# Squares, high-part products and weight splits in the pooling mixer of a two-block network

## The chip, the cores and the metric

The kernel runs on one core of a Trainium2 chip. Its time is the device time of one execution in microseconds; a figure for a kernel is the median of its runs. Each kernel has one profiled execution besides, and all times inside the kernel are on that execution's clock, counted from the start of its span.

## The reference

Two blocks of layers follow each other on 256 tokens of width 1024 in float32. The first block (two layers of mixed attention) isn't touched. The second has two layers; in front of the 256 tokens it puts 16 learned ones, so it works on 272. Its first layer is the stage that matters here:

```python
f = swiglu(rmsnorm(h, ffn_norm_pre[0, 0]), ...)
h = h + 0.5 * rmsnorm(f, ffn_norm_post[0, 0])
hn = rmsnorm(h, mix_norm_pre[0])
m = causal_multiscale_pool(hn, pool_w[0], pool_b[0], pool_scale[0])
h = h + rmsnorm(m, mix_norm_post[0])
f = swiglu(rmsnorm(h, ffn_norm_pre[0, 1]), ...)
```

The pool splits the 1024 channels into four groups of 256. Group g takes, for each token, the mean over the last 2, 4, 8 or 16 tokens, subtracts the token itself, and multiplies the difference by a 256 x 256 matrix of its own. A bias is added and a scale per channel applied.

## The kernel before

Activations lie with channels on the 128 partitions and the 272 tokens along the row: the state is eight tiles `h[0..7]`, and a product's operand is eight pairs `xh[k]`, `xl[k]`. A float32 value is split in a high part (`xh`, `hi`) that TensorE reads in its fast float32 form, and a low part (`xl`, `lo`), the rest. A product of two such values is three products: low weight by high operand, high weight by high operand, and high weight by low operand.

Weights come in chunks of 128 x 1024, in the order in which they are used. SyncE's queue loads a chunk into one of four `raw` buffers (L233); ScalarE casts it to `hi` (L250) and VectorE subtracts to get `lo` (L251). Both together are called a split. Near a border between stages splits are held back (`held`) and issued later by `release`, which asks the scheduler to place them behind given instructions. Each engine runs its instructions in the order that a scheduler gave them when the program was built; `issue_after` is a wish for that order.

Between a feed-forward layer and the pool stands `boundary` (from L941). It has the sums of squares of the layer's output, makes the scale `s` from them (logarithm and exponential on ScalarE, in two halves of the tokens), and then makes the tiles one after the other: VectorE multiplies the layer's output `fg[k]` by `s` (L958, L964) and adds it to `h[k]` (L972); ScalarE makes `xh[k]` (L387) and VectorE `xl[k]` (L388). Tile 0 has a shorter way: VectorE makes its `xh` directly (L965), and `xl` (L969) follows behind the addition to `h` (L968). The squares of `h`, wanted for the norm ahead of the pool, are made by ScalarE: those of tiles 0, 2 and 4 into `sums`, those of 1, 3 and 5 into `sq`, which GpSimd adds to the former (L979); tiles 6 and 7 have `sums` of their own.

`pool_mixer` (from L1122) multiplies first and takes the means afterwards. For each of the eight tiles it makes nine products: three token tiles (128, 128 and 16 tokens) by the three products of parts, with the tile as the stationary operand (L287 low part of the tile, L288 low part of the weights, L289 both high). The results are rows by token; two groups, so four tiles, fill one set of three PSUM banks, and each set is copied to `zt` in SBUF (L1185, L1187). Between the tiles TensorE sums the squares over channels with a matrix of 1/1024 (`squares`, L1163): a set is three products of 2 columns, one for each token tile, and each is seen as two passes. When the last set is done, ScalarE makes the scale of the norm from it by logarithm and exponential (`rt_pool`, `rc_pool`, L934 and L935), and `bands` multiplies the banded matrices of the means by it: `mb[0]` (L1214) and `mb[2]` (L1218) on VectorE, `mb[1]` (L1216) on ScalarE. Then comes the mix: for each of the eight channel tiles three products of `zt` by these matrices (L1195, L1197, L1199) bring the data back to channels on partitions, and `branch_out` evicts the bank: ScalarE takes the squares (`facc`, `fq`, L1015), VectorE the values (`fg`, L1016). GpSimd adds the squares of the first five tiles (L1021) into `facc`. Four products with the matrix of means (L1031) add all of it, over tile 5, `facc`, tile 6 and tile 7 in that order, and the next boundary starts with its scale.

Two splits are released in the middle of the tiles, behind the last `xl` (`self.tiles_done`); in the trace they run on ScalarE and VectorE while TensorE is at tiles 5 to 7.

## Time and profile before

| | |
|---|---|
| runs | 1266.91, 1268.29, 1268.59 us |
| median | 1268.29 us |
| profiled execution | 1266.44 us, span 1264.7 us |
| mean granted TensorE clock | 0.995 |
| TensorE busy | 1237.0 us, 98% of the span |
| VectorE, ScalarE, GpSimd busy | 850.3, 699.6, 204.7 us |
| read from HBM | 200.16 MB, 159 GB/s over the span |

Busy times overlap, and a busy TensorE isn't always at its peak. The stage of the pool mixer is read in the timelines: each row has the start, the time, engine, line and operation, output <- input with their shapes, and in brackets how long the engine had been idle before it and what released it. Rows of one line that follow each other are merged (x6); their time then runs from the first start to the last end. Float32 products of full width, as in the sums of squares, stand as two passes each.

### The profile page before, as it was taken

The numbers are of one execution on the slowest core, as the hardware profiler recorded it, in microseconds if no ns is written. First come the engines' busy times: TensorE is split into PE (matmuls) and PEld (weight loads), VectorE is DVE, ScalarE is ACT, GpSimd is POOL, SyncE is SP. The second block draws the span as 40 slices with busy tenths as digits, with TensorE's granted clock in tenths as the row PEclk, the third lists the DMA queues.
The fourth block names the chain that finished last, engine by engine and source line by source line (L and its number), as shares of the span: only waits on it lengthen the run. The fifth ranks groups of instructions, "written<-read, shape, count | busy, mean of one in ns | idle before, by whom it ended". The sixth has DMA issues, their size and how long they took to land.

```text
span 1264.7 us, 23255 instructions
## 1 busy us (share of the span) xinstructions
PE 1237.0 (98%) x9105; PEld 1161.2 (92%) x9105; DVE 850.3 (67%) x1468; ACT 699.6 (55%) x1233; POOL 204.7 (16%) x308
## 2 busy tenths in 40 slices
PE   8999999999999999899999999999999999999998
PEld 6778897789999999799999999999999988999986
DVE  7988759777666644887664467665456886776652
ACT  6878658586544533565444346444335665665541
POOL 5201010012211112321111122110121002321100
PEclk9999999999999999999999999999999999999999
DMA  7642443335554554146555526554534533475550
GB/s 261 202 160 91 167 167 115 119 125 179 202 179 168 182 167 167 34 139 228 171 180 169 182 84 218 186 181 173 178 117 152 166 117 118 153 240 176 185 181 34
DMA packets 59662, 202.72 MB, mean 160 GB/s; under 512 B 7456, under 2 KB 10656, under 8 KB 59552
## 3 DMA queue, kind: packets, MB, share of 16 engines
q1 hardware_dynamic: 59120, 200.58, 46.7%
q8 instruction: 71, 1.16, 0.4%
q10 hardware_dynamic: 432, 0.66, 0.1%
q14 instruction: 39, 0.32, 0.1%
HBM read 200.16 MB, written 1.05 MB: 159 GB/s over the span
## 4 chain that ended last, share of the span: by engine, by line
PE 91%; DVE 4%; ACT 3%; DMA 1%; issue 1%; SPq 0%; POOL 0%; DVEq 0%; ACTq 0%
PE mm L287 23%; PE mm L288 23%; PE mm L289 23%; PE mm L301 2%; PE mm L304 2%; PE mm L302 2%; PE mb L287 1%; DMA raw<-in_w_dram 1%; PE mb L288 1%; PE mb L289 1%; DVE lo L251 1%; ACT hi L250 1%; PE gl L896 1%; PE gl L287 1%; PE gl L289 1%
## 5 line engine op out<-in xcount | busy, mean ns | idle before, releaser
L251 DVE TENSOR_TENSOR lo<-raw,hi 128x1024 fp32r<-128x1024 f32 (+1 forms) x376 | 470.2, 1256 | 241.8 <-ACT hi L250 241.2
L250 ACT CAST hi<-raw 128x1024 fp32r<-128x1024 f32 (+1 forms) x376 | 390.1, 1044 | 336.7 <-PE mm L289 294.5
L287 PE MATMUL mm<-xh,lo 128*128 128x272 f32 (+1 forms) x1520 | 437.8, 288 | 0.1
L288 PE MATMUL mm<-xl,hi 128*128 128x272 f32 (+1 forms) x1520 | 435.8, 287 | 0.0
L289 PE MATMUL mm<-xh,hi 128*128 128x272 f32 (+1 forms) x1520 | 434.8, 286 | 0.0
L287 PEld LDWEIGHTS mm<-xh,lo 128*128 128x128 f32 x1520 | 286.5, 188 | 2.7 <-issue 1.6
L289 PEld LDWEIGHTS mm<-xh,hi 128*128 128x128 f32 x1520 | 286.4, 188 | 0.9 <-issue 0.8
L288 PEld LDWEIGHTS mm<-xl,hi 128*128 128x128 f32 x1520 | 285.9, 188 | 0.7 <-issue 0.4
L287 PE MATMUL mm<-fh,lo 128*128 128x272 f32 x528 | 152.1, 288 | 0.0
L288 PE MATMUL mm<-fl,hi 128*128 128x272 f32 x528 | 152.0, 288 | 0.0
L289 PE MATMUL mm<-fh,hi 128*128 128x272 f32 x528 | 151.5, 287 | 0.0
L1048 POOL TENSOR_TENSOR a<-a,b 128x272 f32<-128x272 f32 (+1 forms) x88 | 79.1, 899 | 410.3 <-DVE b L1047 368.8
L287 PEld LDWEIGHTS mm<-fh,lo 128*128 128x128 f32 x528 | 99.3, 188 | 0.0
L289 PEld LDWEIGHTS mm<-fh,hi 128*128 128x128 f32 x528 | 99.3, 188 | 0.0
L288 PEld LDWEIGHTS mm<-fl,hi 128*128 128x128 f32 x528 | 99.3, 188 | 0.0
L1021 POOL TENSOR_TENSOR facc<-facc,fq 128x272 f32<-128x272 f32 (+1 forms) x28 | 26.4, 941 | 274.0 <-ACT fq L1011 264.4
L383 ACT CAST fh<-a 128x272 fp32r<-128x272 f32 (+1 forms) x88 | 36.8, 418 | 54.6 <-POOL a L1048 54.6
L301 PE MATMUL mm<-xh,lo 128*128 128x272 f32 (+1 forms) x208 | 56.1, 300 | 8.8 <-DVE xh L965 8.6
L1047 DVE TENSOR_TENSOR b<-mm,r 128x272 f32<-128x272 f32 (+1 forms) x88 | 38.3, 435 | 39.1 <-PE mm L289 37.2
L302 PE MATMUL mm<-xh,hi 128*128 128x272 f32 (+1 forms) x208 | 54.5, 292 | 0.0
L1045 DVE TENSOR_TENSOR a<-mm,r 128x272 f32<-128x272 f32 (+1 forms) x88 | 38.2, 435 | 19.3 <-PE mm L289 10.3
L301 PEld LDWEIGHTS mm<-xh,lo 128*128 128x128 f32 x208 | 40.2, 193 | 10.0 <-DVE xh L965 6.8
(386 smaller groups left out, 1932.4 us busy)
## 6 DMA issues: line engine op xcount, KB each, us to landing
raw<-in_w_dram SPq DMA_DIRECT2D x372, 512.0 KB, 3.3
raw<-in_w_dram SPq DMA_DIRECT2D x4, 256.0 KB, 5.2
memt<-in_memt_dram SPq DMA_DIRECT2D x1, 1024.0 KB, 7.7
memt<-in_memt_dram SPq DMA_DIRECT2D x2, 512.0 KB, 4.5
h<-in_xt_dram SPq DMA_DIRECT2D x7, 128.0 KB, 5.4
grow<-in_grow_dram SPq DMA_DIRECT2D x1, 512.0 KB, 5.9
out_dram<-fgr ACTq DMA_DIRECT2D x2, 256.0 KB, 2.1
out_dram<-fgr SPq DMA_DIRECT2D x2, 256.0 KB, 2.0
```

The costliest lines, as they stand in the source:

```text
L250: nc.scalar.copy(hi[:, s], raw[:, s])
L251: nc.vector.tensor_sub(lo[:, s], raw[:, s], hi[:, s].bitcast(F32))
L287: mm(out, a[1], b[0], start=start, stop=False)
L288: mm(out, a[0], b[1], start=False, stop=False)
L289: self.last_mm = mm(out, a[0], b[0], start=False, stop=stop)
L301: mm(out, w[1], x[0], start=start, stop=False)
L302: mm(out, w[0], x[0], start=False, stop=False)
L383: self.nc.scalar.copy(hi, x)
L1021: nc.gpsimd.tensor_add(R(st["acc"]), R(st["acc"]), R(q))
L1045: nc.vector.tensor_mul(a, pa[:, :n], r[:, lo:])
L1047: last = nc.vector.tensor_mul(b, pb[:, :n], r[:, lo:])
L1048: nc.gpsimd.tensor_mul(a, a, b)
```

## The change

All of it lies in `boundary`, `pool_mixer` and `bands`. ScalarE now writes the squares of every tile to a `sums` tile of its own, GpSimd adds none, and TensorE takes eight sets of squares instead of five. For each tile the six products with `xh` come first, for all three token tiles, and the three with `xl` follow. The copies of the first three banks to `zt` are asked for behind the last tile, those of the second three behind `mb[0]`. The two splits are released one at a time, behind all three scaled matrices, in the mix at the row tiles 1 and 3.

```diff
--- before.py
+++ after.py
@@ -973,13 +973,8 @@
                 ins = self.split_scaled(R(self.xh[k]), R(self.xl[k]), R(h), g(k))
                 self.tiles_done = ins
             if cols:
-                if k < KD - 2 and k % 2:
-                    q = W("sq", 2)
-                    nc.scalar.activation(q, h, AF.Square)
-                    nc.gpsimd.tensor_add(sums[-1], sums[-1], q)
-                else:
-                    sums.append(cols.tile([128, L2], F32, name=self.nm("sums"), tag=f"sums{k}"))
-                    nc.scalar.activation(sums[-1], h, AF.Square)
+                sums.append(cols.tile([128, L2], F32, name=self.nm("sums"), tag=f"sums{k}"))
+                nc.scalar.activation(sums[-1], h, AF.Square)
             elif k == 0:
                 nc.scalar.activation(R(acc), R(h), AF.Square)
             else:
@@ -1170,23 +1165,32 @@
                     for k in range(2):
                         w = self.take(2, "pool_w_2")
                         c = 2 * g + k
+                        mm = nc.tensor.matmul
                         for t, n, ts in toks:
-                            self.mm3(ps[t][0:n, o:o + 256], (self.xh[c][:, ts], self.xl[c][:, ts]), w, k == 0, k == 1)
-                        if c in (2, 4, 5, 6):
-                            squares({2: 0, 4: 1, 5: 2, 6: 3}[c])
-                            if c == 6:
-                                self.release(self.tiles_done, 2)
-                                squares(4)
-                                bands = self.bands(pp, ph, m1, m0f)
-                                next(bands)
-                for t, n, ts in toks:
-                    d = zt[0:n, t, 512 * b:512 * b + 512]
-                    if t == 1 and b == 1:
-                        nc.vector.tensor_copy(d, ps[t][0:n, :])
-                    else:
-                        nc.scalar.copy(d, ps[t][0:n, :])
-                    if b == 1:
-                        next(bands, None)
+                            p, x = ps[t][0:n, o:o + 256], self.xh[c][:, ts]
+                            mm(p, x, w[1], start=k == 0, stop=False)
+                            mm(p, x, w[0], start=False, stop=False)
+                        for t, n, ts in toks:
+                            mm(ps[t][0:n, o:o + 256], self.xl[c][:, ts], w[0], start=False, stop=k == 1)
+                        if 1 < c < 7:
+                            squares(c - 2)
+                        if c == 6:
+                            squares(5)
+                            squares(6)
+                            squares(7)
+                            bands = self.bands(pp, ph, m1, m0f)
+                            done = [next(bands)]
+                with ExitStack() as ctx:
+                    for i in done if b else self.tiles_done:
+                        ctx.enter_context(self.tc.issue_after(i.ins))
+                    for t, n, ts in toks:
+                        d = zt[0:n, t, 512 * b:512 * b + 512]
+                        if t == 1 and b == 1:
+                            nc.vector.tensor_copy(d, ps[t][0:n, :])
+                        else:
+                            nc.scalar.copy(d, ps[t][0:n, :])
+                        if b == 1 and t < 2:
+                            done.append(next(bands))
             mb = self.mb
             for m in range(KD):
                 g = m // 2
@@ -1198,6 +1202,8 @@
                                  skip_group_check=True)
                 nc.tensor.matmul(ps[:, 0:32], zt[:, 2, f], mb[2][:, g, :], start=False, stop=True,
                                  skip_group_check=True)
+                if m in (1, 3):
+                    self.release(done, 1)
                 self.branch_out(ps[:, :L2], m, None, None, 0, st,
                                 (self.gv("pool_scale_2", (0,), m), bs[:, 0, m:m + 1], bs[:, 1, m:m + 1],
                                  bs[:, 2, m:m + 1]), 3)
@@ -1211,11 +1217,9 @@
         v = ph[:, 0:6].rearrange("p (t two) -> p t two", two=2)[:, :, 0]
         self.rsq(rc, v, self.eps, rt)
         self.mb = [pp.tile([128, 4, n], F32, name=f"mb{n}") for n in (144, 128, 32)]
-        nc.vector.tensor_scalar(self.mb[0], m1, rc[:, 0:1], None, op0=OP.mult)
-        yield
-        nc.scalar.activation(self.mb[1], m1[:, :, 0:128], AF.Copy, scale=rc[:, 1:2])
-        yield
-        nc.vector.tensor_scalar(self.mb[2], m0, rc[:, 2:3], None, op0=OP.mult)
+        yield nc.vector.tensor_scalar(self.mb[0], m1, rc[:, 0:1], None, op0=OP.mult)
+        yield nc.scalar.activation(self.mb[1], m1[:, :, 0:128], AF.Copy, scale=rc[:, 1:2])
+        yield nc.vector.tensor_scalar(self.mb[2], m0, rc[:, 2:3], None, op0=OP.mult)
 
     def diff_attention(self, scale):
         nc, t2 = self.nc, self.t2
```

On TensorE, at the end of the sixth tile and the start of the seventh (numbered from 0; `xl6`, `xh7` are parts of tiles, `ss` the sums of squares, `mm` the banks, ending 23, 24, 25 for the three token tiles). Before:

```order
L289 MATMUL mm_1157_6225<-hi_1110_5840,xh6_89 16x256
L1163 MATMUL ss_1148_6173<-mean_133,sums_1146_6165 128x2 x3
L1163 MATMUL ss_1148_6173<-mean_133,sums_1147_6171 128x2 x3
L287 MATMUL mm_1155_6223<-hi_1110_5840,xl7_98 128x256
L288 MATMUL mm_1155_6223<-lo_1111_5841,xh7_90 128x256
L289 MATMUL mm_1155_6223<-hi_1110_5840,xh7_90 128x256
L287 MATMUL mm_1156_6224<-hi_1110_5840,xl7_98 128x256
L288 MATMUL mm_1156_6224<-lo_1111_5841,xh7_90 128x256
```

and after the change:

```order
L1174 MATMUL mm_1157_6225<-hi_1110_5840,xl6_97 16x256
L1158 MATMUL ss_1148_6170<-mean_133,sums_1144_6150 128x2 x3
L1158 MATMUL ss_1148_6170<-mean_133,sums_1145_6156 128x2 x3
L1158 MATMUL ss_1148_6170<-mean_133,sums_1146_6162 128x2 x3
L1158 MATMUL ss_1148_6170<-mean_133,sums_1147_6168 128x2 x3
L1171 MATMUL mm_1155_6223<-lo_1111_5841,xh7_90 128x256
L1172 MATMUL mm_1155_6223<-hi_1110_5840,xh7_90 128x256
L1171 MATMUL mm_1156_6224<-lo_1111_5841,xh7_90 128x256
L1172 MATMUL mm_1156_6224<-hi_1110_5840,xh7_90 128x256
L1171 MATMUL mm_1157_6225<-lo_1111_5841,xh7_90 16x256
L1172 MATMUL mm_1157_6225<-hi_1110_5840,xh7_90 16x256
L1174 MATMUL mm_1155_6223<-hi_1110_5840,xl7_98 128x256
```

Four sets of squares instead of two stand ahead of tile 7, and the first bank's last product is the seventh of the tile instead of the third.

On ScalarE, from the last tile to the evictions of the mix (`rc_pool` is the exponential, `mb128` the second scaled matrix, `facc` the first eviction, `hi` a cast of weights). Before:

```order
L250 CAST hi_1131_6002<-raw_1130_6000 128x1024
L250 CAST hi_1153_6179<-raw_1152_6177 128x1024
L934 ACTIVATE rt_pool_6273<-ss_1148_6173,eps_127 128x3
L1187 COPY zt_6048<-mm_1155_6223 128x512
L935 ACTIVATE rc_pool_6274<-rt_pool_6273 128x3
L1187 COPY zt_6048<-mm_1157_6225 16x512
L1216 ACTIVATE mb128_6278<-m1_6045,rc_pool_6274 128x512
L1015 ACTIVATE facc_1163_6300<-mm_1161_6295,bs_6108,vec_72 128x272
L1015 ACTIVATE fq_1166_6308<-mm_1164_6303,bs_6108,vec_72 128x272
L1015 ACTIVATE fq_1169_6317<-mm_1167_6312,bs_6108,vec_72 128x272
L1015 ACTIVATE fq_1172_6326<-mm_1170_6321,bs_6108,vec_72 128x272
```

and after:

```order
L934 ACTIVATE rt_pool_6275<-ss_1148_6170,eps_127 128x3
L1191 COPY zt_6048<-mm_1155_6223 128x512
L935 ACTIVATE rc_pool_6276<-rt_pool_6275 128x3
L1191 COPY zt_6048<-mm_1157_6225 16x512
L1221 ACTIVATE mb128_6280<-m1_6045,rc_pool_6276 128x512
L250 CAST hi_1131_6002<-raw_1130_6000 128x1024
L1010 ACTIVATE facc_1163_6302<-mm_1161_6297,bs_6108,vec_72 128x272
L1010 ACTIVATE fq_1166_6312<-mm_1164_6305,bs_6108,vec_72 128x272
L1010 ACTIVATE fq_1169_6321<-mm_1167_6316,bs_6108,vec_72 128x272
L250 CAST hi_1153_6176<-raw_1152_6174 128x1024
L1010 ACTIVATE fq_1172_6332<-mm_1170_6325,bs_6108,vec_72 128x272
```

The two casts move from ahead of the logarithm to behind `mb128` and behind the third eviction; the copy of bank 23 stays between logarithm and exponential.

On VectorE at the same place (`lo` is the subtraction of a split, `fg` an eviction). Before:

```order
L251 TENSOR_TENSOR lo_1132_6003<-raw_1130_6000,hi_1131_6002 128x1024
L251 TENSOR_TENSOR lo_1154_6180<-raw_1152_6177,hi_1153_6179 128x1024
L1214 TENSOR_SCALAR mb144_6277<-m1_6045,rc_pool_6274 128x576
L1185 COPY zt_6048<-mm_1156_6224 128x512
L1218 TENSOR_SCALAR mb32_6279<-m0_6046,rc_pool_6274 128x128
L1016 TENSOR_SCALAR fg0_1162_6299<-mm_1161_6295,bs_6108 128x272
L1016 TENSOR_SCALAR fg1_1165_6307<-mm_1164_6303,bs_6108 128x272
L1016 TENSOR_SCALAR fg2_1168_6316<-mm_1167_6312,bs_6108 128x272
L1016 TENSOR_SCALAR fg3_1171_6325<-mm_1170_6321,bs_6108 128x272
```

and after:

```order
L1220 TENSOR_SCALAR mb144_6279<-m1_6045,rc_pool_6276 128x576
L1189 COPY zt_6048<-mm_1156_6224 128x512
L1222 TENSOR_SCALAR mb32_6281<-m0_6046,rc_pool_6276 128x128
L251 TENSOR_TENSOR lo_1132_6003<-raw_1130_6000,hi_1131_6002 128x1024
L1011 TENSOR_SCALAR fg0_1162_6301<-mm_1161_6297,bs_6108 128x272
L1011 TENSOR_SCALAR fg1_1165_6311<-mm_1164_6305,bs_6108 128x272
L1011 TENSOR_SCALAR fg2_1168_6320<-mm_1167_6316,bs_6108 128x272
L251 TENSOR_TENSOR lo_1154_6177<-raw_1152_6174,hi_1153_6176 128x1024
L1011 TENSOR_SCALAR fg3_1171_6331<-mm_1170_6325,bs_6108 128x272
```

The subtractions move from ahead of the first scaled matrix to ahead of the first and of the fourth eviction.

## Rows read from the trace of the kernel before

**Rows 1.** Timeline, TensorE, the pool mixer; columns as described above.

```profile
508.32 0.58 PE L287 MATMUL mm<-hi,xl 128*128 128x256 f32 x1 [3.49 <-DVE xl L969]
508.70 0.41 PE L288 MATMUL mm<-lo,xh 128*128 128x256 f32 x1
...
514.14 0.39 PE L287 MATMUL mm<-hi,xl 128*128 128x256 f32 x1
...
516.33 0.73 PE L1163 MATMUL ss<-mean,sums 128*128 128x2 f32 x6
517.70 0.61 PE L1163 MATMUL ss<-mean,sums 128*128 128x2 f32 x4 [0.64 <-POOL sums L979]
...
520.58 1.40 PE L1163 MATMUL ss<-mean,sums 128*128 128x2 f32 x12
521.84 0.36 PE L287 MATMUL mm<-hi,xl 128*128 128x256 f32 x1
...
523.84 0.39 PE L1195 MATMUL mm<-mb,zt 128*128 128x144 f32 x1 [0.70 <-DVE mb L1214]
524.43 0.49 PE L1197 MATMUL mm<-mb,zt 128*128 128x128 f32 x2
...
529.74 0.70 PE L1031 MATMUL ss<-fq,mean 128*128 128x272 f32 x2
530.28 0.62 PE L1031 MATMUL ss<-facc,mean 128*128 128x272 f32 x2
...
534.07 0.36 PE L301 MATMUL mm<-xh,lo 128*128 128x272 f32 x1 [2.25 <-DVE xh L965]
```

**Rows 2.** Windows: length, busy PE, PEld, DVE, ACT, POOL, granted clock, DMA share, GB/s.

```profile
507.00:512.00 5.00, 3.67 (x16) 3.02 (x17) 5.00 (x11) 2.12 (x5) 4.65 (x25) 0.66 0.00 0
512.00:518.00 6.00, 5.36 (x46) 4.81 (x44) 6.00 (x15) 4.88 (x13) 2.23 (x2) 1.00 0.00 0
```

**Rows 3.** Timeline, VectorE, one stretch of the feed-forward layer and the pool mixer.

```profile
462.77 1.23 DVE L251 TENSOR_TENSOR lo<-raw,hi 128x1024 fp32r<-128x1024 f32 x1 [1.77 <-ACT hi L250]
...
509.88 0.69 DVE L388 SCALAR_TENSOR_TENSOR xl<-h,vec,xh 128x272 fp32r<-128x272 f32 x1
...
510.85 1.18 DVE L972 TENSOR_TENSOR h<-h,fg 128x272 f32<-128x272 f32 x1
...
513.08 1.01 DVE L388 SCALAR_TENSOR_TENSOR xl<-h,vec,xh 128x272 fp32r<-128x272 f32 x1
...
517.73 0.90 DVE L388 SCALAR_TENSOR_TENSOR xl<-h,vec,xh 128x272 fp32r<-128x272 f32 x2
...
526.18 2.17 DVE L1016 TENSOR_SCALAR fg<-mm,bs 128x272 f32<-128x272 f32 x4 [1.59 <-ACT facc L1015]
...
532.61 0.30 DVE L964 TENSOR_TENSOR fg<-fg,s 128x136 f32<-128x136 f32 x1 [1.44 <-ACT s L951]
```

**Rows 4.** Timeline, GpSimd, the same stretches.

```profile
463.17 1.45 POOL L1021 TENSOR_TENSOR facc<-facc,fq 128x272 f32<-128x272 f32 x1 [7.50 <-ACT fq L1011]
...
510.97 0.76 POOL L979 TENSOR_TENSOR sums<-sums,sq 128x272 f32<-128x272 f32 x1
512.99 0.80 POOL L979 TENSOR_TENSOR sums<-sums,sq 128x272 f32<-128x272 f32 x1 [1.26 <-ACT sq L978]
...
526.69 3.27 POOL L1021 TENSOR_TENSOR facc<-facc,fq 128x272 f32<-128x272 f32 x4 [9.04 <-ACT fq L1015]
```

**Rows 5.** Timeline, ScalarE, the end of the pool mixer and after it.

```profile
522.47 0.59 ACT L1187 COPY zt<-mm 128x512 f32<-128x512 f32 x1 [0.20 <-PE mm L289]
522.96 0.21 ACT L935 ACTIVATE rc_pool<-rt_pool 128x3 f32<-128x3 f32 x1
...
525.57 0.58 ACT L1015 ACTIVATE facc<-mm,bs,vec 128x272 f32<-128x272 f32 x1 [1.19 <-PE mm L1199]
...
545.23 2.94 ACT L250 CAST hi<-raw 128x1024 fp32r<-128x1024 f32 x3
```

**Rows 6.** Weight loads issued between 515 and 546 us.

```profile
DMA to landing us min/median/max: 3.3/3.8/4.3
```

## Prediction, made before the changed kernel ran

> **What bounds the kernel now.** I read TensorE's timeline first, in the 30 us between the last product of one feed-forward layer and the first of the next. Elsewhere TensorE is almost never idle, and the change touches nothing else. The reader is to see three gaps in [rows 1]: 3.49 us before the first pool product at 508.32 (it waits for xl of tile 0, VectorE), 0.64 us before 517.70 (GpSimd's add of two tiles' squares), and 0.70 us before 523.84 (VectorE's scaled band matrix). Second, the windows: in 507 to 512 the granted clock is 0.66, in 512 to 518 it is 1.00 [rows 2]; a 256-column product lasts 0.58 and 0.41 us at first [rows 1]. Third, the timelines of VectorE, GpSimd and ScalarE, for what those gaps wait for. VectorE makes the tiles until 518.63, and two of its instructions stand out: the h add at 510.85 takes 1.18 us and the xl at 513.08 takes 1.01, where two xl at 517.73 take 0.90 together [rows 3]. Both run while GpSimd adds squares, 510.97 to 511.73 and 512.99 to 513.79 [rows 4], and both end 0.30 us after it.
>
> So two limits take turns: VectorE's tiles set the pace at first, then TensorE is behind (18 products from 514.14 to 516.33, 0.122 us each), and after the last squares a chain ScalarE, VectorE, TensorE sets the start of the mix at 523.84. The stage ends with four sums of squares from 529.74 on, of which GpSimd's accumulator is the second, at 530.28; scale and first tile follow, to 534.07 [rows 1].
>
> **The change part by part.** Times are on the clock of the profiled execution (1266.44 us, span 1264.7); the median of the three runs is 1268.29, 1.85 above it, and the sum's difference is added to each.
>
> *High parts first.* The first products wait no longer for xl of tile 0, which VectorE makes behind the h add, but for its xh. The next layer's entrance has that pattern already: 2.25 us of idling instead of 3.49, and a product of 0.36 us instead of 0.58 behind it [rows 1]. So TensorE starts 1.2 us earlier, near 507.2. But tile 1 comes no earlier (its xl ends at 509.88 + 0.69 = 510.57 [rows 3]), so TensorE empties its queue and waits again: nothing on the path, except that tile 0's squares fit in that hole.
>
> *Squares without sums.* Three GpSimd adds go. VectorE can win up to 1.18 - 0.45 = 0.73 us at the h add and 0.56 at the xl; I take 1.1 for both, since another GpSimd step still precedes the first. TensorE is behind by then, so the sum uses none of it.
>
> The Trainium skill (SBUF — State Buffer, Who interferes with whom) says that a VectorE instruction with two SBUF inputs and a GpSimd instruction that reads SBUF exclude each other for a whole instruction. The two long rows agree. By that rule the later tiles come 1.1 us earlier, without it no earlier; the same rule speaks against another part of the change, below.
>
> On TensorE five sets of squares become eight. Two sets (twelve passes) take 521.84 - 520.58 = 1.26 us [rows 1], so a set is 0.63, and I add 0.09 where products follow. From the end of xl 1, 510.62 with the hand-over, TensorE has no more gap: 3 products of tile 1 and 45 of tiles 2 to 6 at 0.122, 5.86 us; the sets of tiles 1, 2, 3 and then four in a row, 7 x 0.63 + 3 x 0.09 = 4.68. Tile 7's products start at 510.62 + 5.86 + 4.68 = 521.16, against 521.84 today: **-0.68**. The start is earlier and the wait for GpSimd is gone, and three more sets (1.9 us) eat most of it. Bounds: +0.9 if the clock is low through tile 1 and its squares as it is today; -0.5 more if square passes overlap better between products. VectorE's last xl ended at 518.63 even before [rows 3], so it isn't awaited.
>
> *Chain to the mix.* Today the mix starts 2.00 us after tile 7's first product. ScalarE's queue has the copy of token tile 0's second half (522.47) ahead of the exponential (522.96) [rows 5], and the order below keeps it so. That copy waits for token tile 0's products of tile 7: three today, seven after, because the low parts come last. Four products at 0.12 are **+0.48**: the mix starts at 523.84 - 0.68 + 0.48 = 523.64. TensorE then issues three products with the first band matrix ahead of the first with ScalarE's, for which it waited 0.3 us before 524.43: **-0.3**. The end of the mix goes from 529.74 to 529.24.
>
> *Rows leave PSUM behind the tiles.* Three ScalarE copies of the first half move from between tiles 4 to 7 to behind tile 7. They are wanted only at the mix, and ScalarE has the time in which it now casts weights: 0. Were that cover gone, each would cost one eviction, 0.58.
>
> *Splits between the evictions.* Two casts (2.94 / 3 = 0.98 us each [rows 5]) and two lo subtractions (1.23 [rows 3]) move behind the start of the mix. The first cast fits into ScalarE's idle 1.19 us before its first eviction at 525.57 [rows 5]. The second stands between the third and the fourth. ScalarE takes 0.58 per eviction and TensorE 0.70 per row tile, so the last eviction ends near 530.6, which is early enough: 0 on ScalarE itself. Behind it wait the second lo on VectorE and GpSimd's accumulator, four adds in 3.27 us from 526.69 [rows 4]. The casts end at 525.1 and 527.9, the evictions between them at 525.8, 526.4 and 526.9; the next one ends at 528.4, and the third add wants it, while lo runs from 527.95 to 529.2. The trace has this pair: a lo at 462.77 for 1.23 us [rows 3], and an accumulator add at 463.17 that takes 1.45 [rows 4] and ends 0.62 after the lo. So add 3 ends at 529.8, add 4 at 530.6, and the accumulator's sum starts at 530.65 instead of 530.28, **+0.37**; from there to the scale nothing changes. The bound below, no blocking, has the adds end at 530.0 and the sum start at 530.05, -0.23. On VectorE 2.46 us of subtractions enter a stretch with 1.59 us idle before its first eviction and 1.44 before the scale [rows 3], so the scale still finds it free by 0.5 us. The loads that wait for the two raw buffers start up to 7.5 us later, after 529.2, land 3.8 us behind that [rows 6], and the next cast is at 545.23 [rows 5]: hidden by 12 us.
>
> **Sum.** The stage's end follows the accumulator: +0.37, since what was won before it is spent waiting for it. 1266.44 + 0.4 = 1266.8 for a run like the profiled one, 1268.29 + 0.4 = **1268.7** for the median.
>
> **Rivals.**
> 1. *GpSimd isn't blocked*, or the second lo falls between two adds. Then the end moves with the mix or with free adds, -0.50 to -0.23: 1267.8 to 1268.1. For it: the four adds of today, with no lo beside them, take 0.82 each. Against: the pair at 463.
> 2. *The tiles set the pace, TensorE isn't behind.* VectorE's last xl would end at 518.63 - 1.1 = 517.5, tile 7's products start at 517.7 instead of 521.84, less 0.5 in chain and tail: about -3.6, 1264.7. For it: gaps of 3.49 and 0.64 us. Against: 0.63 us per set and 0.122 per product add up to 10.5 us after 510.6.
> 3. *The clock stays low* in the pool products. The products start after 2.25 us of idling instead of 3.49, but then TensorE waits for tile 1 in holes up to 0.6 us. If it stays at 1.2 GHz up to tile 7, 63 products take 0.24 instead of 0.122 and 48 square passes between 0.105 and 0.21: from 507.2 on 15.1 + 5.0 to 10.1 us, so tile 7 starts at 527.3 to 532.4 and the kernel ends 6 to 11 us later, about 1276. It decides once the clock is low beyond 513, where TensorE is behind. Against it: 3.67 busy of 5 us brought the clock back today, and 5.36 of 6 kept it at 1.00 [rows 2]. The Trainium skill (TensorE: Matmul & The Clock Gate, Part 1) calls the throttled state the default that activity releases, so by it every hole is a risk; it gives this rival its place, not its time.
> 4. *The splits end up on the path*: ScalarE and VectorE bound the mix, not TensorE. Then 2 x 0.98 - 1.19 + 0.37, about +1.2: 1269.5.
>
> **Chances.** Forecast 0.42, rival 1 0.25, rival 4 0.18, rival 2 0.06, rival 3 0.05, something that I don't see 0.04. 0.2% of this kernel, about what a measurement can tell from no change, is 2.5 us: the forecast and rivals 1 and 4 lie inside it. So 0.85 for no change that can be told, 0.07 faster (rival 2 and a part of the unseen), 0.08 slower (rival 3 and the rest). With the ends of the terms, -1.2 (both the overlap of square passes and free adds) and +1.3 (low clock, and the blocked adds), around runs that scatter by 1.7 us (1266.91 to 1268.59), the range is 1266.3 to 1270.0.
>
> **What the next profile would show.** The first pool product near 507.2, lasting about 0.36 us; no gap on TensorE from tile 2 to tile 7; 48 square passes; VectorE's h add and xl at 0.4 to 0.5; tile 7's first product near 521.2, the first mix near 523.6; a GpSimd accumulator add of 1.3 us or more beside the second lo; the accumulator's sum near 530.6; the next layer's first product near 534.4. I am wrong if tile 7 starts before 520 or after 523, if the clock is below 1.00 in 512 to 524, or if the last sums don't wait for the accumulator.

## The result and the profile after

The changed kernel takes 1276.06 us (median of 6 runs, 1274.28 to 1277.58), the kernel before 1267.95 (6 runs beside it, 1266.91 to 1269.14): ratio 1.0059, 95% interval 1.0048 to 1.0071. It is 8.1 us slower, and the time lies outside the range of the prediction.

The profiled execution took 1277.58 us (span 1275.8, mean granted clock 0.984), against 1266.44 (1264.7, 0.995) before: 11.1 us of span to account for, more than the medians differ. The first view is the windows of the changed kernel, in the columns of [rows 2] (the granted clock is the last but two):

```profile
507.00:512.00 5.00, 5.00 (x26) 4.46 (x27) 5.00 (x12) 2.53 (x7) 3.71 (x23) 0.59 0.00 0
512.00:518.00 6.00, 6.00 (x29) 5.44 (x30) 4.80 (x13) 4.68 (x12) 0.00 (x0) 0.50 0.00 0
518.00:524.00 6.00, 6.00 (x55) 5.84 (x53) 0.00 (x0) 0.23 (x1) 0.00 (x0) 0.99 0.01 3
524.00:532.00 8.00, 7.02 (x36) 6.40 (x36) 3.65 (x6) 4.43 (x9) 0.51 (x1) 0.56 0.12 34
532.00:538.00 6.00, 6.00 (x36) 5.80 (x35) 4.35 (x8) 3.99 (x7) 3.03 (x4) 0.73 0.34 129
```

The same view of the kernel before, for the stretches that [rows 2] doesn't hold:

```profile
518.00:524.00 6.00, 5.29 (x45) 4.83 (x45) 3.72 (x6) 4.22 (x9) 0.00 (x0) 1.00 0.38 107
524.00:532.00 8.00, 7.75 (x58) 7.10 (x58) 4.88 (x10) 4.92 (x10) 3.04 (x4) 1.00 0.14 53
```

In 512 to 518 TensorE is busy all the time, at a clock of 0.50, where it had 1.00 before: 29 instructions stand in this window instead of 46. In 518 to 524 the clock is back, and in 524 to 532 it is low again. The kernel before has a low stretch at the entrance too (0.66 in 507 to 512, [rows 2]); new are that it lasts until 518 and that a second one follows. A full "busy" says nothing of the speed here. TensorE's timeline shows where the clock turns (columns as in [rows 1]):

```profile
506.88 0.38 PE L1171 MATMUL mm<-lo,xh 128*128 128x256 f32 x1 [2.25 <-DVE xh L965]
...
507.80 1.36 PE L1158 MATMUL ss<-mean,sums 128*128 128x2 f32 x6
...
509.81 0.41 PE L1171 MATMUL mm<-lo,xh 128*128 128x256 f32 x1
...
511.73 1.27 PE L1158 MATMUL ss<-mean,sums 128*128 128x2 f32 x6
...
518.50 0.72 PE L1158 MATMUL ss<-mean,sums 128*128 128x2 f32 x6
...
521.95 2.73 PE L1158 MATMUL ss<-mean,sums 128*128 128x2 f32 x24
524.55 0.36 PE L1171 MATMUL mm<-lo,xh 128*128 128x256 f32 x1
524.75 0.28 PE L1172 MATMUL mm<-hi,xh 128*128 128x256 f32 x1
524.87 0.32 PE L1171 MATMUL mm<-lo,xh 128*128 128x256 f32 x1
524.99 0.41 PE L1172 MATMUL mm<-hi,xh 128*128 128x256 f32 x1
...
527.45 1.80 PE L1199 MATMUL mm<-mb,zt 128*128 128x144 f32 x6 [0.98 <-DVE mb L1220]
...
536.73 0.71 PE L1026 MATMUL ss<-fq,mean 128*128 128x272 f32 x2
537.27 0.62 PE L1026 MATMUL ss<-facc,mean 128*128 128x272 f32 x2
...
541.05 0.37 PE L301 MATMUL mm<-xh,lo 128*128 128x272 f32 x1 [2.24 <-DVE xh L965]
```

A 256-column product that lasts 0.28 us in a queue at 2.4 GHz lasts 0.41 at 1.2, and a set of six square passes 0.72 or 1.27. So the clock falls inside the first set of squares, comes back by 518.5, and falls again at 525, behind the run of 24 square passes, without an idle moment there. The next table shows where the difference arises, from the starts of the same work in the two traces:

| | before | after | delay so far |
|---|---|---|---|
| first pool product | 508.32 | 506.88 | -1.4 |
| tile 7's first product | 521.84 | 524.55 | +2.7 |
| first product of the mix | 523.84 | 527.45 | +3.6 |
| sums of squares behind the mix | 529.74 | 536.73 | +7.0 |
| first product of the next layer | 534.07 | 541.05 | +7.0 |

The changed kernel was 0.2 us ahead when the stage began (the feed-forward layer's last sums of squares started at 503.30 instead of 503.50), so 1.2 of the 1.4 us belong to the change. Of the 7.0 us, 2.7 have arisen by tile 7, 0.9 in the chain to the mix, and 3.4 in the mix.

1.5 us more come before 942, mostly from another low stretch (542.0 to 545.4) just behind the next layer's first products, and 2.6 at the entrance of a later stage, at 1079: 0.8 of them in a longer wait (2.91 us instead of 2.11), the rest behind it, where the clock was 0.88 in 1080 to 1100, against 1.00 before. The change has no instruction there.

VectorE's timeline (columns as in [rows 3]), with two h adds, an xl, the last tile's xl, and the second lo of the splits:

```profile
510.27 0.81 DVE L972 TENSOR_TENSOR h<-h,fg 128x272 f32<-128x272 f32 x2
512.13 0.49 DVE L388 SCALAR_TENSOR_TENSOR xl<-h,vec,xh 128x272 fp32r<-128x272 f32 x1
516.53 0.50 DVE L388 SCALAR_TENSOR_TENSOR xl<-h,vec,xh 128x272 fp32r<-128x272 f32 x1 [0.23 <-ACT xh L387]
533.23 1.23 DVE L251 TENSOR_TENSOR lo<-raw,hi 128x1024 fp32r<-128x1024 f32 x1 [0.37 <-ACT hi L250]
```

The h adds take 0.4 us each (one took 1.18 in [rows 3]), the xl 0.49 (1.01 there), and the last tile is done at 517.03 instead of 518.63. TensorE is behind VectorE by then (it is at tile 4), and is what the stage waits for. The lo stands between the evictions, as the change asks.

### The profile page after: what moved, and what is told of

The parts are those of the page before. It is cut to its first block, busy times and chain, and to the rows that moved or that the text cites. A ratio compares the mean times of both kernels' runs of the same rounds, so it can differ in the third digit from the quotient of the medians.

```text
span 1275.8 us, 23287 instructions
## 1 busy us (share of the span) xinstructions
PE 1248.9 (98%) x9123; PEld 1174.0 (92%) x9123; DVE 850.2 (67%) x1468; ACT 699.8 (55%) x1233; POOL 202.8 (16%) x305
## 4 chain that ended last, share of the span: by engine, by line
PE 91%; DVE 3%; ACT 3%; DMA 1%; issue 1%; SPq 0%; DVEq 0%; ACTq 0%
PE mm L287 23%; PE mm L288 23%; PE mm L289 23%; PE mm L301 2%; PE mm L304 2%; PE mm L302 2%; PE mb L287 1%; DMA raw<-in_w_dram 1%; PE mb L289 1%; PE mb L288 1%; DVE lo L251 1%; ACT hi L250 1%; PE gl L896 1%; PE gl L287 1%; PE gl L289 1%
## 5 line engine op out<-in xcount | busy, mean ns | idle before, releaser
L1043 POOL TENSOR_TENSOR a<-a,b 128x272 f32<-128x272 f32 (+1 forms) x88 | 76.4, 868 | 417.2 <-DVE b L1042 366.9
```

The costliest lines, as they stand in the source:

```text
L1043: nc.gpsimd.tensor_mul(a, a, b)
```

## Every run, by its clock

Before the experiments, one reading of all runs. Each run has a mean granted clock. In the 29 runs of the kernel before that stood beside four of the experiments (splits only, high parts only, 3 and 4), time goes with it: 1265.62 us at 0.995, 1268.33 (the median) at 0.992, 1274.36 at 0.989. With TensorE busy for 98% of the span, time x clock should be nearly constant, and it is: the median of time - 1275 x (1 - clock) is 1258.9 us for these runs. The same figure for the changed kernel is 1258.2, at a median clock of 0.9865, and for the twelve other kernels below 1257.9 to 1261.1; the three highest of these (1260.1, 1260.1 and 1261.1) have squares of 128 columns. The clock is given to 0.001, so such a figure is good to about 0.6 us. At one clock the two kernels take the same time; 1275 x (0.993 - 0.9865) = 8.3 us is the whole difference. This says that the loss goes with the clock, not yet what lowers the clock.

## Experiments

The theories that the expectations name: **S**, the many square passes of 2 columns bring the clock down; **E**, it is the entrance, where the products start on tile 0 alone and TensorE then waits for tile 1; **W**, the added work and the new order cost the time and the clock only follows. Later, inside S: **S1**, the run of 24 passes ahead of tile 7 is the cause; **S2**, it is the number of such passes among the products, wherever they stand. The first four expectations say C for the clock as the cause, entrance and passes not yet divided; O, in the run of experiment 5, is the theory that ScalarE's order alone made the run of experiment 4 fast. Ratios are to the kernel before on the same chip, with 95% intervals. The groups of runs stood on different chips (medians of the kernel before 1267.79 to 1268.33), so a difference of two medians is good to about half a microsecond.

**1. The parts of the change, each by itself.** Only the copies and splits moved, squares and products as before:

```diff
-                                self.release(self.tiles_done, 2)
...
+                    for i in done if b else self.tiles_done:
+                        ctx.enter_context(self.tc.issue_after(i.ins))
...
+                if m in (1, 3):
+                    self.release(done, 1)
```

> The kernel before with only the copies of rows and the two splits moved, as in the change; squares and the order of products as before. Theory C: tiles and clock as before, the accumulator's sum late by 0.4 us, so 1267.5 to 1269.5. Theory W: the splits bound the mix, 1270 or more, with ScalarE or VectorE as what the last sums wait for.

1268.54 us (10 runs), ratio 1.0006 (0.9997 to 1.0016), median clock 0.9925: no change.

Only the high parts first:

```diff
-                            self.mm3(ps[t][0:n, o:o + 256], (self.xh[c][:, ts], self.xl[c][:, ts]), w, k == 0, k == 1)
...
+                            mm(p, x, w[1], start=k == 0, stop=False)
+                            mm(p, x, w[0], start=False, stop=False)
+                        for t, n, ts in toks:
+                            mm(ps[t][0:n, o:o + 256], self.xl[c][:, ts], w[0], start=False, stop=k == 1)
```

> The kernel before with only the high parts first; five sets of squares and GpSimd's adds as before. Theory C: TensorE starts after 2.25 us of idling; with no set of squares in the first hole the clock may hold (1266.5 to 1268.5) or fall as in the changed kernel (1270 to 1275), and time follows the clock: each microsecond at half clock beyond tile 2 costs about 0.5 us. Theory W: 1268 to 1269, whatever the clock does.

1266.31 us (10 runs), ratio 0.9987 (0.9970 to 1.0005), clock 0.994. The early entrance by itself costs nothing, which speaks against E.

Only the eight sets of squares (GpSimd's three adds go with them):

```diff
...
-                        if c in (2, 4, 5, 6):
-                            squares({2: 0, 4: 1, 5: 2, 6: 3}[c])
...
+                        if 1 < c < 7:
+                            squares(c - 2)
+                        if c == 6:
...
+                            squares(5)
+                            squares(6)
+                            squares(7)
...
```

> The kernel before with only the squares changed: a tile of squares for each tile, eight sets of 2-column products on TensorE, none of GpSimd's adds; low parts first, splits and copies where they were. Theory S (the eight sets keep TensorE's clock low, by themselves): mean clock 0.990 or less and 1272 to 1276 us. Theory E (the early entrance with its holes does it): 1267 to 1269 at the clock of before, 0.992 to 0.994.

1276.91 us (4 runs), ratio 1.0069 (1.0052 to 1.0086), clock 0.985: the whole loss, without the rest of the change. That it is the passes and not the missing adds is for experiment 4, which has no adds either. Its windows:

```profile
512.00:516.00 4.00, 4.00 (x21) 3.79 (x20) 3.29 (x9) 1.58 (x5) 0.00 (x0) 0.50 0.00 0
520.00:524.00 4.00, 4.00 (x37) 3.84 (x36) 2.54 (x4) 3.30 (x6) 0.00 (x0) 1.00 0.00 0
524.00:528.00 4.00, 3.33 (x27) 2.96 (x27) 1.62 (x3) 1.90 (x5) 0.00 (x0) 0.85 0.75 246
528.00:532.00 4.00, 4.00 (x19) 3.88 (x19) 1.46 (x4) 1.30 (x3) 0.56 (x1) 0.50 0.04 16
```

And the change without the eight sets, with GpSimd's three adds back:

```diff
...
-                        if 1 < c < 7:
-                            squares(c - 2)
...
+                        if c in (2, 4, 5, 6):
+                            squares({2: 0, 4: 1, 5: 2, 6: 3}[c])
...
```

> The changed kernel with the squares of before (three adds on GpSimd, five sets): high parts first, copies and splits moved. Theory S: the clock of before or better, 1266 to 1268.5. Theory E: 1272 to 1276.

1268.47 us (10 runs), ratio 1.0005 (0.9988 to 1.0022), clock 0.9925. Its windows, with the clock back by 512 and up to the end of the stage:

```profile
508.00:512.00 4.00, 3.64 (x16) 2.49 (x16) 4.00 (x8) 1.83 (x5) 3.43 (x8) 0.57 0.00 0
512.00:516.00 4.00, 4.00 (x37) 3.81 (x37) 4.00 (x10) 2.38 (x6) 0.86 (x2) 1.00 0.00 0
524.00:528.00 4.00, 4.00 (x37) 4.00 (x37) 3.96 (x6) 3.88 (x8) 2.38 (x3) 1.00 0.35 131
```

**2. The eight sets without the early entrance**: the change with the low parts first, as before.

```diff
...
-                            mm(p, x, w[1], start=k == 0, stop=False)
...
+                            self.mm3(ps[t][0:n, o:o + 256], (self.xh[c][:, ts], self.xl[c][:, ts]), w, k == 0, k == 1)
```

> The changed kernel with the low parts first again, as before: eight sets, copies and splits moved. TensorE then starts after 3.5 us of idling and without a set of squares in a hole behind the start. Theory S: still slow, 1271 to 1276, since the long run of 24 passes stays. Theory E: 1267 to 1270.

1276.01 us (4 runs), ratio 1.0057 (1.0039 to 1.0075). The loss stays without the early entrance: E falls. The entrance isn't quite that of the kernel before, though: here, as in the run with the eight sets alone, the set of tile 0 was put ahead of the first product (at 508.48, behind 3.17 us of idling).

A single profile must be read with care: the profiled executions of the kernels with only the high parts first (1273.26 us) and with only the splits moved (1270.44 us) are the slowest of their ten, and show the low clock as the changed kernel does: from 509 to 519, and again from 526, about 2 us behind their run of 12 passes, around a wait ahead of the mix (1.17 and 0.71 us). What the eight sets do is turn such executions from the exception into the rule.

**3. A warm entrance**: eight bf16 products of 128 x 512 without use between the last sums of the feed-forward layer and the first pool product, to keep TensorE at work there.

```diff
...
+            with self.tc.issue_after(self.last_pss.ins):
+                self.warm("mm", 8)
             ph = self.bank("ss")
```

> The changed kernel with eight dummy products (128 x 512, bfloat16) on TensorE in the idle stretch between the last sum of squares of the feed-forward layer and the first pool product; nothing else moves on any engine. Theory C (the changed kernel loses its time to TensorE's low clock, because the entrance's idling is now followed by short products, holes and 2-column square passes): the granted clock stays at 1.00 at least to tile 4, tile 7 starts near 521 as forecast, and the time is 1267 to 1271, more only if the 24 square passes ahead of tile 7 bring the clock down by themselves. Theory W (the extra sets of squares, the delayed copy and the splits among the evictions cost the time, at any clock): 1275 to 1277, as without the dummies.

1273.34 us (8 runs, 1268.82 to 1276.81), ratio 1.0031 (1.0009 to 1.0053), clock 0.9885. It gets back 2.7 of the 8.1 us by the medians, 3.6 of 7.5 by the ratios; with these intervals that is rough. Its timeline around the run of 24 passes, in its fastest run:

```profile
516.51 0.50 PE L1177 MATMUL mm<-hi,xl 128*128 128x256 f32 x3
516.85 2.73 PE L1161 MATMUL ss<-mean,sums 128*128 128x2 f32 x24
519.44 0.54 PE L1174 MATMUL mm<-lo,xh 128*128 128x256 f32 x1
519.78 0.42 PE L1175 MATMUL mm<-hi,xh 128*128 128x256 f32 x1
```

The clock was 1.00 from 504 to 516, three products ahead of the run take 0.50 us, and right behind it one takes 0.42. No idle time stands in between. The time that theory C had expected (1267 to 1271) was missed: I had taken the entrance for the whole of it, and the clock falls behind the run of passes even when the entrance was warm.

**4. The same squares, 128 columns wide.** Each product sums the squares into 128 equal columns instead of 2.

```diff
-                    nc.tensor.matmul(ph[:, 2 * t:2 * t + 2], sums[j][:, a:a + 128], self.mean[:, 0:2],
+                    nc.tensor.matmul(ph[:, 128 * t:128 * t + 128], sums[j][:, a:a + 128], self.mean[:, 0:128],
...
```

> The changed kernel with 128 columns of the matrix of means in each square product instead of 2 (same values, 128 times over); the passes take no less time, the scheduler also puts the exponential ahead of the copy on ScalarE, which is worth 0.5 us. Theory C: the square passes now count as work, the clock stays at 1.00 or falls for at most one short stretch at the entrance, 1266.5 to 1270. Theory W: TensorE does the same passes or longer ones, 1275 to 1277.

1268.77 us (10 runs), ratio 1.0002 (0.9992 to 1.0013), clock 0.993: the loss is gone, with 48 passes as before. The place to compare with the last fence:

```profile
518.13 0.51 PE L1174 MATMUL mm<-hi,xl 128*128 128x256 f32 x3
518.48 2.84 PE L1158 MATMUL ss<-mean,sums 128*128 128x128 f32 x24
521.08 0.36 PE L1171 MATMUL mm<-lo,xh 128*128 128x256 f32 x1
521.28 0.28 PE L1172 MATMUL mm<-hi,xh 128*128 128x256 f32 x1
```

The 24 passes take 2.84 us instead of 2.73, so TensorE is no less and no longer busy, and the products behind them last 0.28: the clock stays there. That is against W: the work is the same or a little more, and the loss is gone. But the scheduler had, with this edit, also put the exponential and the second scaled matrix ahead of the second half's copies on ScalarE, and had broken up two of the early sets (4 passes and 2 instead of 6), so the columns weren't all that had changed.

Nor do 128 columns keep the clock everywhere. This profile (1272.82 us, the slowest of its ten) has it low at the entrance, and again from 530.6 to 540.9, from just behind the wait for GpSimd's accumulator into the next layer:

```profile
506.71 0.58 PE L1171 MATMUL mm<-lo,xh 128*128 128x256 f32 x1 [2.25 <-DVE xh L965]
```

**5. The exponential first, alone**, with 2 columns:

```diff
...
-                    for i in done if b else self.tiles_done:
+                    for i in done + [self.rsq_last] if b else self.tiles_done:
```

> The changed kernel with only ScalarE's exponential (and the second scaled matrix) ahead of the copies of the second rows, as the scheduler had it in the run with 128 columns; 2 columns as in the change. Theory S: the order on ScalarE is worth 0.5 to 1 us and no more, 1274.5 to 1276.5, mean clock 0.988 or less. Theory O (that order, not the columns, made the run with 128 columns fast): 1267.5 to 1270.

1271.93 us (10 runs), ratio 1.0030 (1.0019 to 1.0041), clock 0.9895. I had expected 0.5 to 1 us of it; it gives 4.1 of the 8.1, and experiment 4 another 3.2 (to 1268.77; the two ratios' intervals don't overlap; by the ratios 3.7 and 3.6 of 7.5). The columns are the main difference between the two runs, not the only one: here the first copy still stands ahead of the second scaled matrix, and the early sets are whole. So the 3.2 us aren't shown to be the columns' alone. The order ends TensorE's hole ahead of the mix:

```profile
522.73 2.73 PE L1158 MATMUL ss<-mean,sums 128*128 128x2 f32 x24
525.33 0.36 PE L1171 MATMUL mm<-lo,xh 128*128 128x256 f32 x1
525.53 0.35 PE L1172 MATMUL mm<-hi,xh 128*128 128x256 f32 x1
525.68 0.41 PE L1171 MATMUL mm<-lo,xh 128*128 128x256 f32 x1
...
527.17 1.64 PE L1199 MATMUL mm<-mb,zt 128*128 128x144 f32 x6
528.61 0.58 PE L1201 MATMUL mm<-mb,zt 128*128 128x128 f32 x2
529.03 0.31 PE L1203 MATMUL mm<-mb,zt 128*128 128x32 f32 x2
```

The clock falls behind the 24 passes all the same (0.41 at 525.68), but no wait stands ahead of the mix at 527.17, where the changed kernel waits 0.98, and by 529.1 it is back (0.31 for a pair of 32 columns, which takes 0.47 at 1.2 GHz). In the changed kernel it stayed low to about 535.

**6. The sets spread out**, one behind each tile and the last two behind tile 7, so that no run is longer than 12 passes.

```diff
-                        if 1 < c < 7:
-                            squares(c - 2)
...
+                        if c:
+                            squares(c - 1)
+                        if c == 7:
...
```

> The changed kernel with its eight sets of 2-column squares spread out: one set behind each tile, and the last two behind tile 7, so that no run is longer than 12 passes, as in the kernel before; 48 passes as in the change. Theory S1 (the run of 24 passes ahead of tile 7 is what keeps the clock low): 1267 to 1270. Theory S2 (the number of such passes among few products does, wherever they stand): 1273 to 1277.

1274.65 us (10 runs, 1270.33 to 1284.52), ratio 1.0056 (1.0031 to 1.0081). S1 falls as the only cause: without the run of 24 the kernel is about as slow. Its runs lie far apart: three at 1283 to 1285 with a clock of 0.979, the other seven at 1270 to 1277. The two sets behind tile 7 also lengthen the chain to the mix (a wait of 1.54 us ahead of it in the profile), and no run tells their share. In the profiled execution (1284.52 us, the slowest) the clock didn't come back from 508 to 545:

```profile
516.00:520.00 4.00, 4.00 (x21) 3.65 (x20) 1.04 (x3) 2.48 (x7) 0.00 (x0) 0.50 0.02 4
540.00:544.00 4.00, 4.00 (x19) 4.00 (x19) 1.68 (x3) 1.67 (x4) 1.52 (x2) 0.50 0.22 84
```

**7. Combinations.** The change with 128 columns and the eight products of experiment 3:

```diff
+                self.warm("mm", 8)
...
+                    nc.tensor.matmul(ph[:, 128 * t:128 * t + 128], sums[j][:, a:a + 128], self.mean[:, 0:128],
```

> The changed kernel with 128 columns in its square products and eight dummy products in the idle stretch at the entrance. Theory S: the clock stays at 1.00 through the stage in most executions, 1265.5 to 1268, some 1 to 2 us below the run with 128 columns alone. If the dummies do nothing for the clock, or set a later fall in its place, 1268 to 1270.

1269.26 us (10 runs), ratio 1.0008 (0.9994 to 1.0021), clock 0.994. The expected 1265.5 to 1268 was missed: the clock is up, and what is left is work: at one clock this kernel is 2.2 us above the kernel before (1261.1 against 1258.9). The sums behind the mix wait for GpSimd's accumulator:

```profile
531.27 0.73 PE L1026 MATMUL ss<-facc,mean 128*128 128x272 f32 x2 [1.20 <-POOL facc L1016]
```

The kernel before with the high parts first and its five sets 128 columns wide (here too the exponential comes ahead of the copies):

```diff
+                            mm(p, x, w[1], start=k == 0, stop=False)
+                            mm(p, x, w[0], start=False, stop=False)
...
+                    nc.tensor.matmul(ph[:, 128 * t:128 * t + 128], sums[j][:, a:a + 128], self.mean[:, 0:128],
```

> The kernel before with the high parts first and 128 columns in each of its five sets' square products; the exponential goes ahead of the copy on ScalarE (0.5 us) and the copies of the first rows go behind the tiles, both by the scheduler. Theory S: the clock falls less often than in the kernel before, mean clock 0.995 or more, 1264 to 1266. Theory E: the clock as with the high parts alone, 1266 to 1268.

1266.08 us (10 runs), ratio 0.9983 (0.9968 to 0.9998). The windows of its profile, again the slowest of its ten (1271.82 us), show the clock low at the entrance although every set is 128 columns wide:

```profile
508.00:512.00 4.00, 3.47 (x15) 2.34 (x16) 4.00 (x9) 1.27 (x3) 3.94 (x24) 0.63 0.00 0
512.00:516.00 4.00, 3.85 (x19) 3.16 (x18) 4.00 (x8) 2.52 (x6) 1.79 (x3) 0.52 0.00 0
```

And the same with the eight products at the entrance:

```diff
+            with self.tc.issue_after(self.last_pss.ins):
+                self.warm("mm", 8)
...
```

> A version meant to beat both kernels: the kernel before with high parts first, five sets of 128-column squares, and eight dummy products at the entrance. Theory S: mean clock 0.995 or more, 1264 to 1266. If the dummies do nothing, as without them, 1266 to 1266.5; if they cost more than they give, 1267 or more.

1266.48 us (12 runs), ratio 0.9986 (0.9975 to 0.9997). Both beat the kernel before by about 0.15%, an interval that only just leaves out no change; the products at the entrance add nothing to the time, and the 1264 to 1266 that both expectations had hoped for were missed. In the last profile the clock is 1.00 from 504 to 548, through sets that are 128 columns wide:

```profile
508.00:512.00 4.00, 2.50 (x14) 1.59 (x15) 4.00 (x8) 1.69 (x5) 3.57 (x8) 1.00 0.00 0
520.00:524.00 4.00, 2.71 (x23) 2.41 (x23) 3.58 (x5) 3.23 (x7) 0.00 (x0) 1.00 0.35 118
```

TensorE is busy for 2.50 and 2.71 of 4 us there, less than in any row of the changed kernel with a clock of 0.50.

## Why the prediction was wrong

**The step that failed** is the cost of three more sets of squares: "a set is 0.63", taken at the full clock, with only 0.9 us as the bound of a low clock, and nothing for a low clock behind tile 7. The sizes were right for that clock (the four sets ahead of tile 7 took 524.55 - 521.95 = 2.60 us, 0.65 each), but with eight sets the clock was low around them. Tile 7 was to come 0.68 us earlier and came 2.71 later, and the mix, forecast at 5.6 us (523.64 to 529.24), lasted 9.3. The stage ended 7.0 us later, for 0.37 forecast. The range was too narrow above in any case: its upper end, 1268.7 + 1.3 = 1270.0, leaves nothing for the scatter of the runs, while its lower end goes 1.2 us below 1268.7 - 1.2. All three signs of being wrong came: tile 7 started after 523, the clock was 0.50 in 512 to 518, and the last sums didn't wait for the accumulator.

A low clock had been written down as the third rival, with its beginning (low beyond 513, where TensorE is behind) and about the right price, 1276; its chance of 0.05 was the mistake. That the price fits is in part luck: the rival blamed the holes at the entrance, kept the clock low up to tile 7 and let it start at 527.3 or later. It started at 524.55, at a clock that had come back, and the second fall, behind tile 7, made up the rest. Its 0.24 us for a product at the low clock was too high as well: in both traces such products start 0.21 us apart (508.70, 508.92 and 509.13 in the kernel before). The argument against the rival was "3.67 busy of 5 us brought the clock back", read from a stretch of 256-column products, and the added passes were counted as busy time like these. The runs show that they aren't alike: eight sets of 2 columns 1276.91, five 1268.47, eight of 128 columns in about the same busy time 1268.77 (this last with the changed orders of experiment 4).

Behind that stands the Trainium skill (TensorE: Matmul & The Clock Gate, Part 1), which calls the throttled state the default that activity releases. The trace agrees as far as it goes: in the changed kernel the clock fell behind a wait of 2.25 us and came back by 518.5, while TensorE was at work. It adds that TensorE can be busy throughout and the clock stay low: 6.00 of 6 us at 0.50 in 512 to 518.

**High parts first**: right. First product at 506.88 (near 507.2 forecast, and 0.2 of the difference lies ahead of the stage), 0.38 us long.

**GpSimd's adds gone**: right, and larger than taken: the last xl ends 1.6 us earlier, 1.4 without the 0.2 ahead of the stage, for 1.1 taken. The rule of the Trainium skill (SBUF — State Buffer, Who interferes with whom) had pointed to this; the rows agree (1.18 to 0.4, 1.01 to 0.49), and as forecast the gain isn't on the path.

**TensorE without a gap from tile 2 to tile 7, 48 passes**: right.

**Chain to the mix**: tile 7's first product to the first mix is 2.90 us, forecast 2.48. The copy stays ahead of the exponential, as forecast:

```profile
524.73 0.26 ACT L934 ACTIVATE rt_pool<-ss,eps 128x3 f32<-128x3 f32 x1 [6.50 <-PE ss L1158]
526.08 0.59 ACT L1191 COPY zt<-mm 128x512 f32<-128x512 f32 x1 [1.09 <-PE mm L1174]
526.56 0.21 ACT L935 ACTIVATE rc_pool<-rt_pool 128x3 f32<-128x3 f32 x1
```

I had priced this order at half a microsecond. Experiment 5 shows that it was worth about 4. The timelines suggest why, without showing it: without the hole ahead of the mix the clock is back by 529, with it at 535.

**Rows behind the tiles**: right, the three copies run at 516.72 while TensorE works.

**Splits and the accumulator**: the mechanism was right, but not on the path in the changed kernel. One add of the accumulator takes 1.25 us beside the second lo (1.3 or more forecast), and yet the sums don't wait for it, as the mix lasts 9.3 us instead of 5.9:

```profile
L1016 POOL TENSOR_TENSOR facc<-facc,fq x4: 757/762/1255, 531.5 to 535.2; 128x272 f32<-128x272 f32 x4
```

The three numbers are the shortest, the median and the longest add, in ns. Where the clock is up they do: 0.32 us in experiment 3, 0.33 with the splits alone, 0.47 in the change with five sets and in experiment 2, 0.68 in experiment 5, 1.19 and 1.20 with eight sets of 128 columns. The forecast of 0.37 was near the lower end.

**No change in the work**: right. At one clock the kernels differ by -0.7 us, about what the clock's rounding leaves open.

Open: whether it is the columns of a pass that count, and how few are too few, since only 2 and 128 were run, and not with all else equal; why one execution of the same kernel loses the clock and the next doesn't; and whether the low stretches later in the kernel (1080 to 1100) belong to the change.

## What to carry to other kernels

Where TensorE is the bound, compare runs at their mean granted clock first: if time - span x (1 - clock) agrees, the work is the same, and the cause is what TensorE does, not how much. Before adding short passes to a stage where TensorE waits at its entrance, count them as busy time that need not keep the clock, and price the stage at half speed with more than a token chance. A hole closed in front of the next block of products, or passes made wider at about the same duration, can be worth more than the instructions saved: here about 4 us (experiment 5), and 3 to 4 more with the columns and the orders that came with them (experiment 4), where three sets of squares take 1.9 us at the full clock.

## What the runs showed of the hardware that was not expected

- A float32 pass of 2 columns and one of 128 take nearly the same time: 24 of them 2.73 and 2.84 us.
- A run of 24 two-column passes was followed by the low clock within 0.7 us in all four profiles that have one and the clock full ahead of it; in both profiles with 24 passes of 128 columns the clock stayed full behind the run.
- The kernel before varies with the clock on its own: 1265.62 us at 0.995 to 1274.36 at 0.989 in 29 runs, three of them above 1273.
- Idle time alone didn't decide: 2.25 us of it ahead of the pool was followed by the clock falling in the changed kernel, and in the kernel before's own next layer (534.07, [rows 1]) it was not. In the changed kernel's next layer (541.05, 2.24 us) it was again, although full products of 272 columns came behind it.
